# Six leading up-projection units instead of four, earlier squares of the second rows, and GpSimd's two-input sums on VectorE

## The chip, the cores and the metric

One core of one Trainium2 chip runs the whole kernel. The metric is the device time of one execution in microseconds. Before the change it is 2574.07 us (median of three runs, 2573.06 to 2575.15). The engines are named as the profile names them: PE is TensorE (PEld its weight loads), DVE is VectorE, ACT is ScalarE, POOL is GpSimd, and SP is SyncE, which issues DMAs.

## The reference

The input x has 2048 positions of 1024 channels, all in float32. There is one layer:

```python
xn = rmsnorm(x, norm1_g)
z = xn @ w_in                         # 1024 -> 512 pool + 4 x 512 HGRN2 + 2048 gates
u_pool, zq, zf, zi, zo, zg = split(z)
gates = sigmoid(zg + b_gate)          # two gates of 1024 channels
ya = pool_mixer(u_pool) @ w_pa        # window means of 2, 4, 8, 16 positions minus the token
yb = hgrn2_mixer(zq, zf, zi, zo) @ w_pb    # chunkwise gated linear recurrence
x = x + (gates[0] * ya + gates[1] * yb) @ w_o
h = rmsnorm(x, norm2_g) @ w_up        # 1024 -> 2 x 2816
hc = causal depthwise convolution of h over 3 positions, + conv_b
x = x + (silu(gate half of hc) * value half of hc) @ w_down
return rmsnorm(x, final_g)
```

## The kernel before

**Passes and products.** The 2048 positions are done in two passes of 1024. A pass consists of `mixer` (input projection, pooling, recurrence, the two branch projections and the output projection `wo`) and `ffn` (up-projection, convolution, gate, down-projection `dn`). Within a pass the positions stand in two blocks of 512. Each large matrix product is done in a two-by-two scheme with seven products P1 to P7 instead of eight: the operands are sums and differences of quarters of the weights and of the activations, and the results are added and subtracted again. Every float32 operand is split into a high part that the matmul takes exactly (ACT or POOL: a cast, `hi`) and the rest (DVE: `lo` is the value minus `hi`), and each step is three matmuls (hi with hi, hi with lo, lo with hi).

**A unit.** In the up-projection a unit m computes one tile of 128 value channels and the tile of 128 gate channels that belongs to it, for both blocks. There are 22 units of seven products, and each product has twelve matmuls over 512 columns. A unit uses three PSUM banks: X for P1 and P2, Z for P6, P7 and P4, V for P5 and P3. `Unit.after` (line 1028) takes the results out: after P1 ACT copies `e1` from X (L1031), after P6 DVE makes `u2` from Z (L1033), after P7 DVE makes `u3` from Z (L1037), and the four results of a unit come after P2, P7, P4 and P3. P4 goes on adding to bank Z, so it cannot begin before `u3` has read that bank.

**Which products can begin.** P1 and P2 need only forms of the pass's first block (B11, B21). P6, P5, P7, P4 and P3 need forms that mix both blocks (T2, T1, T3, T4, B22). These are made by `forms_b_task` (line 678): PE turns the rows of the second block, DVE makes the differences t1, t2 (L712), POOL some of the others (L729, L746), ACT and DVE split each into `hi` (L606) and `lo` (L607). The task starts with `norm_rows`: for each row tile, two squares on ACT with a running sum (L635), the root on POOL (L636, L628, L629) and the scaling on DVE (L649). After that it waits for `go`. In the up-projection `go` is given before the sixth product (`GO_AT = 5`). `up_order` (line 426) writes out the order of the products: with `N_HEADS = 2`, the units 0 and 1 and then 2 and 3 do P1 and P2 first (eight products), then each pair its other five; the remaining units follow, interleaved one product of one unit with one of the next.

**Weights.** `Stream.convert` takes the next weight operand from its raw buffer (eight of these, filled by SP), lets ACT cast `hi` (L205) and DVE make `lo` (L206), up to four products ahead and into six buffers. It calls `load_ahead`, which issues the next raw loads.

**After a unit.** Results wait in a list `work`; one item is taken after each product (`drain(1)`). Items are `conv` (POOL copies two columns of history, L1402 and L1404; ACT the first tap, L1407; DVE two more, L1409 and L1412) and `glu` (ACT the activation L1416; then a product of gate and value: L1418 on DVE for the second block, L1420 for the first block, there on POOL for units 0 to 3 and on DVE for the rest). When two neighbouring units are through, `add_forms` makes their four sums or differences for the down-projection on POOL (`comb`, L1103, named gf); each is stored by a DMA that POOL issues too (L1432). In the down-projection they are fetched again by POOL's queue (L805). The output projection gets its sums in the same way (yf) while the second branch projection (`pb`) runs, without a store.

**Other POOL sums that the change touches.** `pool_task` makes the window sums by doubling (L778): groups 0 and 2 on POOL, groups 1 and 3 on DVE. The last norm multiplies one half row tile of the first block by the gain on POOL (L1484).

**Order and buffers.** The program is traced in Python; a scheduler then fixes one order for each engine from the order of tracing and its own estimates, and at run time each engine goes through its list. `behind` adds an edge that the scheduler must keep. Tiles of 128 x 512 share 82 slots. In the head of the kernel the first block's `forms_a_task` is traced, then the loads of the second block's rows; the second block's `norm_rows` (names x1_0 to x1_3) is traced at the first tick of the matmul count, so after the first weight conversions.

Of the kernel before, what the change touches and what calls it, by code (L numbers as in the profile page):

```python
# [14 lines left out]
AF = mybir.ActivationFunctionType  # L15
ALU = mybir.AluOpType
# [42 lines left out]

N_SLOTS = 82  # L60
N_RUN = 3
N_HEADS = 2
GO_AT = 5
LEAD = 5
X_AT, X_AT2 = 1, 4
GO_IO = (("P2", 1), ("P2", 0))
G_POOL = 4
O_AT, O_LAG = 3, 1
FIN_WAIT = 4
N_RAW = 8  # L70
# [8 lines left out]
def tile_trunk(  # L79
# [32 lines left out]
    def f32(ap):  # L112
        return ap.bitcast(F32)
# [43 lines left out]
    class Stream:  # L157
# [34 lines left out]
        def convert(self):  # L192
            j = len(self.tiles)
            key, fn, raws = self.ops[j]
            while any(r.tile is None for r in raws):
                self.load()
            store_kept()
            v = fn(f"w{j}")
            t = opsp.tile([P, 2, 512], F32R, tag="ops", name=f"ops{j}")
            n = int(np.prod(v.shape[1:]))  # L200
            hi, lo = t[:, 0, :n], t[:, 1, :n]
            if len(v.shape) == 3:
                hi = hi.rearrange("p (a b) -> p a b", a=v.shape[1])
                lo = lo.rearrange("p (a b) -> p a b", a=v.shape[1])
            self.mark = act.copy(hi, v)  # L205
            dve.tensor_tensor(lo, v, f32(hi), ALU.subtract)  # L206
            self.tiles.append((key, t))
            self.load_ahead()
# [24 lines left out]
            mybir.DependencyClass.NoSync, mybir.DependencyReason.DATA), reason="behind")  # L233

    urgent = [None]

    def first(ins):

# [182 lines left out]
        return {p: (lambda p=p: plan(p)) for p in ORDER}  # L421

    def up_order():
        heads = [(0, 1), (2, 3), (4, 5)][:N_HEADS]
        res = [(m, p) for ms in heads for p in ("P1", "P2") for m in ms]
        res += [(m, p) for ms in heads for p in ("P6", "P5", "P7", "P4", "P3") for m in ms]

        rest = [(7 * m + 2 * i, m, p) for m in range(2 * N_HEADS, MF)
                for i, p in enumerate(ORDER)]
        return res + [(m, p) for _, m, p in sorted(rest)]  # L430
# [201 lines left out]
    def row_rstd(halves, junk, name):  # L632
        ss = small.tile([P, 4], F32, tag="ssq", name=name + "ss")
        for hf in range(2):
            act.activation(junk[hf], halves[hf], AF.Square, accum_out=ss[:, hf : hf + 1])  # L635
        pool.tensor_tensor(ss[:, 2:3], ss[:, 0:1], ss[:, 1:2], ALU.add)  # L636
        return rstd_of(ss[:, 2:3], 1, 1.0 / D, name + "r")

# [125 lines left out]


    def pool_task(b, g, u, w_mix, md):
        add = pool if g % 2 == 0 else dve
        w = WINDOWS[g]
        pool.tensor_copy(u[:, 1:16], uhist[:, g, 1:16])
        pool.tensor_copy(uhist[:, g, 1:16], u[:, 513:528])  # L770
        s = u
        k = 1
        lo = 1
        while k < w:
            t = slot(f"s{b}_{g}_{k}", 528)
            lo += k
            a = 16 if 2 * k == w else lo
            add.tensor_tensor(t[:, a:528], s[:, a:528], s[:, a - k : 528 - k], ALU.add)  # L778
            s = t
            k *= 2  # L780
            yield 6
        p = slot(f"p{b}_{g}")
        dve.scalar_tensor_tensor(p, s[:, 16:528], 1.0 / w, u[:, 16:528], ALU.mult, ALU.subtract)
        if b == 0:
            dve.tensor_tensor(p[:, :16], s[:, 16:32], inv[:, g], ALU.mult)
            dve.tensor_tensor(p[:, :16], p[:, :16], u[:, 16:32], ALU.subtract)
        pl = split(p, f"pl{b}_{g}")
        yield 6
        ps = bank(f"pm{b}_{g}")
        c = g * P  # L790
        pe.matmul(ps, w_mix[:, 0, c : c + P], pl[0], start=True, stop=False)
        pe.matmul(ps, w_mix[:, 0, c : c + P], pl[1], start=False, stop=False)
        pe.matmul(ps, w_mix[:, 1, c : c + P], pl[0], start=False, stop=True)
        t = slot(f"mx{b}_{g}")
        act.activation(t, ps, AF.Copy, scale=col(o_ps + g))
        md[b, g] = spill(t, f"md{b}_{g}")
# [300 lines left out]
    def add_forms(two, forms, k, name, store=lambda p, t: None, sums=True, pin=lambda i: None):  # L1097

        def comb(p, x0, x1, op):
            if (p, k) in forms or x0 is None or x1 is None:  # L1100
                return
            t = slot(f"{name}_{p}_{k}")
            pin(pool.tensor_tensor(t, x0, x1, op))  # L1103
            forms[p, k] = t
            store(p, t)

# [273 lines left out]
    def ffn(b0, forms, late):  # L1380
# [15 lines left out]
        def emit_up(m):  # L1396
# [17 lines left out]
            def glu(hf):  # L1414
                g = ts[1, hf]
                in_turn(act.activation(g, g, AF.Silu))  # L1416
                if hf:
                    dve.scalar_tensor_tensor(g, g, -1.0, ts[0, hf], ALU.mult, ALU.mult)  # L1418
                else:
                    (pool if m < G_POOL else dve).tensor_tensor(g, g, ts[0, hf], ALU.mult)  # L1420
                k = m // 2
                two = gp.setdefault(k, {})
                two[hf, m % 2] = g
# [45 lines left out]
        def final(hf, j):  # L1469
# [11 lines left out]
            for c in (1 - hf, hf):  # L1481
                if (hf, c) == (0, 1):
                    act.activation(res[c], halves[c], AF.Copy, scale=r[:, 0:1])
                    pool.tensor_tensor(res[c], res[c], fg[c], ALU.mult)  # L1484
                else:
                    dve.scalar_tensor_tensor(res[c], halves[c], r[:, 0:1], fg[c],
                                             ALU.mult, ALU.mult)
# [61 lines left out]
        nxt[1].step()  # L1549
    load_rows(1)  # L1550
    join(nxt[1])
    Task(setup_task())
    lg = cols[:, o_lb : o_lb + 4]
    dve.tensor_tensor(lbt[:, 0], lg, lg, ALU.subtract)
# [61 lines left out]
```

## Time and profile before

| what | value |
|---|---|
| median of three runs | 2574.07 us |
| profiled execution | 2575.64 us, of which the span is 2573.9 us |
| mean granted clock of TensorE | 0.993 |
| head: up to the end of the combined projection `io` | about 0 to 122 us |
| first pass: rest of the mixer, `wo`, up, down | up begins at 651 us, down at 1093 us |
| second pass | from 1312 us; up begins at 1913 us, down at 2347 us |

How to read the profile: the page gives busy times of the engines over the span. The timeline lists instructions in order of time: start in us, duration in us, engine, line, operation, output<-inputs, count, and in brackets the idle time of that engine just before, with what ended it. The windows view gives, for each stretch, busy us and number of instructions of each engine, the granted clock of TensorE (1.00 is full speed), the busy share of the DMA engines and GB/s. The groups view gives busy us and mean ns of all instructions of one line.

### The profile page before, as it was taken

The page shows a single profiled execution, that of the slowest core. Times are in us where ns is not written, and L with a number is a line of the kernel's source. Part 1 is how long each engine was busy: PE and PEld are TensorE (multiplying, and loading weights), DVE is VectorE, ACT ScalarE, POOL GpSimd, SP SyncE. Part 2 cuts the span into 40 slices and gives each one's busy share as a digit, 9 for nine tenths or more (in the row PEclk, how much of TensorE's full clock was granted, in tenths as well). Part 3 has the DMA queues.
Part 4 walks back from the last instruction along what each step waited for, and adds up shares of the span by engine and source line. Part 5 has one row for each costly group of instructions (what it writes and reads, how often), then busy time and mean ns, then how long its engine had stood idle before and what let it go on. Part 6 is the DMA issues. An engine that isn't in the chain of part 4 may idle for free.

```text
span 2573.9 us, 35491 instructions
## 1 busy us (share of the span) xinstructions
PE 2519.3 (98%) x11464; PEld 2057.0 (80%) x11464; DVE 1964.0 (76%) x3382; ACT 1191.9 (46%) x2244; POOL 851.5 (33%) x1209
## 2 busy tenths in 40 slices
PE   7899999999999999999999999999999999999998
PEld 6678888788788888878878888888887888888887
DVE  7878788478789777786486776775978987778844
ACT  5335434324555544554364354442355554445533
POOL 6534344031445333462141111200223433334502
PEclk9899999999999999999999999999999999999999
DMA  6787768767788888887364343356442454446942
GB/s 219 254 248 204 210 201 247 215 223 245 179 235 235 235 242 230 252 318 252 107 211 149 99 139 119 120 160 224 143 165 88 151 153 144 144 139 209 366 149 98
DMA packets 254058, 496.88 MB, mean 193 GB/s; under 512 B 26736, under 2 KB 43248, under 8 KB 253552
## 3 DMA queue, kind: packets, MB, share of 16 engines
q1 hardware_dynamic: 187968, 319.89, 38.5%
q0 software_dynamic: 41504, 110.64, 16.8%
q10 hardware_dynamic: 24400, 64.08, 7.3%
q8 instruction: 90, 1.47, 0.2%
q14 instruction: 96, 0.79, 0.1%
HBM read 384.94 MB, written 187.17 MB: 222 GB/s over the span
## 4 chain that ended last, share of the span: by engine, by line
PE 89%; DVE 5%; issue 2%; ACT 2%; DMA 1%; POOL 1%; SPq 0%; DVEq 0%; POOLq 0%; ACTq 0%
PE dn_P L145 16%; PE up_Z L145 14%; PE up_V L145 9%; PE up_X L145 9%; PE wo_P L145 6%; PE gr_Z L145 5%; PE pb L145 3%; PE pa L145 3%; PE gr_X L145 3%; PE gr_V L145 3%; PE fr_Z L145 3%; PE fr_V L145 2%; PE fr_X L145 2%; PE pl L867 1%; PE io_Z L145 1%
## 5 line engine op out<-in xcount | busy, mean ns | idle before, releaser
L205 ACT CAST ops<-raw 128x512 fp32r<-128x512 f32 x732 | 452.7, 620 | 792.9 <-PE dn_P L145 147.6
L206 DVE TENSOR_TENSOR ops<-raw,ops 128x512 fp32r<-128x512 f32 x732 | 555.4, 762 | 207.8 <-ACT ops L205 204.0
L1409 DVE SCALAR_TENSOR_TENSOR e<-h,cols,e 128x512 f32<-128x512 f32 x176 | 142.4, 812 | 30.8 <-ACT e L1407 26.5
L1407 ACT ACTIVATE e<-h,cols 128x512 f32<-128x512 f32 x176 | 142.4, 814 | 29.1 <-DVE h L997 21.0
L1412 DVE SCALAR_TENSOR_TENSOR e<-h,cols,e 128x512 f32<-128x512 f32 x176 | 133.7, 768 | 2.8
L805 POOL DMA_DIRECT2D g_P<-dg_P x154 | 83.3, 543 | 101.3 <-PE dn_P L145 28.5
L1103 POOL TENSOR_TENSOR gf_P<-e,e 128x512 f32<-128x512 f32 x44 | 65.6, 1493 | 153.3 <-DVE e L1418 98.8
L1103 POOL TENSOR_TENSOR gf_P<-gf_P,e 128x512 f32<-128x512 f32 x44 | 59.1, 1344 | 66.6 <-DVE e L1418 66.1
L1402 POOL COPY h<-h 128x2 f32<-128x2 f32 x88 | 39.5, 463 | 121.2 <-DVE h L995 119.2
L1404 POOL COPY hist<-h 128x2 f32<-128x2 f32 x88 | 38.8, 442 | 121.1 <-DVE h L997 119.4
L1416 ACT ACTIVATE e<-e 128x512 f32<-128x512 f32 x88 | 55.6, 632 | 46.2 <-DVE e L1412 46.0
L997 DVE TENSOR_TENSOR h<-up_u,up_V 128x512 f32<-128x512 f32 x88 | 60.0, 682 | 13.3 <-PE up_V L145 12.8
L1212 POOL TENSOR_TENSOR q<-q,qs 128x512 f32<-128x512 f32 x16 | 22.7, 1419 | 139.0 <-ACT qs L1211 127.9
L854 POOL COPY qm<-q 128x64 f32<-128x64 f32 x64 | 24.4, 404 | 117.7 <-DVE q L860 43.9
L1079 DVE TENSOR_TENSOR x<-x,wo_P 128x512 f32<-128x512 f32 x88 | 56.0, 675 | 8.3 <-PE wo_P L145 8.1
L1249 ACT ACTIVATE gt<-gt,cols 128x512 f32<-128x512 f32 x48 | 34.8, 725 | 57.5 <-DVE gt L997 35.1
L1079 DVE TENSOR_TENSOR ac<-ac,dn_P 128x512 f32<-128x512 f32 x72 | 47.3, 682 | 18.4 <-PE dn_P L145 16.5
L1103 POOL TENSOR_TENSOR yf_P<-ya,ya 128x512 f32<-128x512 f32 x16 | 21.1, 1322 | 117.3 <-DVE ya L1326 117.3
L628 POOL TENSOR_SCALAR ro<-so 128x4 f32<-128x4 f32 x16 | 3.2, 199 | 156.8 <-ACT junk L969 156.8
L1477 POOL TENSOR_TENSOR fss<-fss 128x1 f32<-128x1 f32 x16 | 6.6, 415 | 144.2 <-ACT fo L1467 144.2
L1432 POOL DMA_DIRECT2D dg_P<-gf_P x88 | 50.1, 569 | 8.5 <-POOL gf_P L1103 7.7
L1031 ACT COPY up_e<-up_X 128x512 f32<-128x512 f32 x44 | 25.8, 586 | 57.6 <-PE up_X L145 47.5
(1267 smaller groups left out, 8303.4 us busy)
## 6 DMA issues: line engine op xcount, KB each, us to landing
g_P<-dg_P POOLq DMA_DIRECT2D x154, 256.0 KB, 6.4
raw<-in_w_up_t SPq DMA_DIRECT2D x132, 256.0 KB, 3.1
raw<-in_w_in_t SPq DMA_DIRECT2D x98, 256.0 KB, 3.2
dg_P<-gf_P POOLq DMA_DIRECT2D x88, 256.0 KB, 3.8
raw<-in_w_io SPq DMA_DIRECT2D x68, 256.0 KB, 4.8
dg_P<-e SPq DMA_DIRECT2D x66, 256.0 KB, 3.2
raw<-in_w_dn SPq DMA_DIRECT2D x66, 256.0 KB, 4.5
x<-in_x SPq DMA_DIRECT2D x64, 256.0 KB, 5.1
```

Source lines behind the costliest of these rows:

```text
L145: count[1] = pe.matmul(*args, **kw)
L205: self.mark = act.copy(hi, v)
L206: dve.tensor_tensor(lo, v, f32(hi), ALU.subtract)
L805: eng.dma_start(t, d)
L997: dve.tensor_tensor(dst, t, ps, ALU.add if how == "add" else ALU.subtract)
L1079: dve.tensor_tensor(t, t, ps[j], ALU.add if sg > 0 else ALU.subtract)
L1103: pin(pool.tensor_tensor(t, x0, x1, op))
L1407: in_turn(act.activation(t, h[:, 2:], AF.Identity, bias=col(o_cb + mt), scale=col(o_cw + 4 * MF + mt)))
L1409: in_turn(second(dve.scalar_tensor_tensor(t, h[:, 1 : 1 + TB], col(o_cw + 2 * MF + mt), t, ALU.mult, ALU.add)))
L1412: dve.scalar_tensor_tensor(t, h[:, 0:TB], col(o_cw + mt), t, ALU.mult, ALU.add)
L1416: in_turn(act.activation(g, g, AF.Silu))
L1432: pool.dma_start(d, t)
```

## The change

Four things are changed.

1. `N_HEADS` is 3: units 0 to 5 do P1 and P2 first (twelve products), then each pair its other five. `GO_AT` stays 5.
2. In the head, the second block's `norm_rows` is traced directly after the first block's forms. The first weight operand that takes a used buffer (number 6 and later) gets an edge: its cast on ACT stands behind the last square of x1_3.
3. `comb` in `add_forms` (L1103, 120 instructions), the window sums of groups 0 and 2 (L778, 16), `glu` of units 0 to 3 for the first block (L1420, 8) and the last norm's product (L1484, 8) go from POOL to DVE.
4. Nothing else: the sums of weights, t3 and t4 of the forms, the history copies and all DMAs that POOL issues stay where they are.

```diff
-N_HEADS = 2
+N_HEADS = 3
...
-G_POOL = 4
...
             self.mark = act.copy(hi, v)
+            if j >= N_OPS and opening[0] is not None:
+                behind(self.mark, opening[0])
+                opening[0] = None
             dve.tensor_tensor(lo, v, f32(hi), ALU.subtract)
...
+    opening = [None]
...
-        heads = [(0, 1), (2, 3), (4, 5)][:N_HEADS]
+        heads = [(0, 1), (2, 3), (4, 5), (6, 7)][:N_HEADS]
...
         for hf in range(2):
-            act.activation(junk[hf], halves[hf], AF.Square, accum_out=ss[:, hf : hf + 1])
+            ins = act.activation(junk[hf], halves[hf], AF.Square, accum_out=ss[:, hf : hf + 1])
+            if name == "x1_3":
+                opening[0] = ins
...
-        add = pool if g % 2 == 0 else dve
...
-            add.tensor_tensor(t[:, a:528], s[:, a:528], s[:, a - k : 528 - k], ALU.add)
+            dve.tensor_tensor(t[:, a:528], s[:, a:528], s[:, a - k : 528 - k], ALU.add)
...
-            pin(pool.tensor_tensor(t, x0, x1, op))
+            pin(dve.tensor_tensor(t, x0, x1, op))
...
-                    (pool if m < G_POOL else dve).tensor_tensor(g, g, ts[0, hf], ALU.mult)
+                    dve.tensor_tensor(g, g, ts[0, hf], ALU.mult)
...
-                    pool.tensor_tensor(res[c], res[c], fg[c], ALU.mult)
+                    dve.tensor_tensor(res[c], res[c], fg[c], ALU.mult)
...
     join(nxt[1])
+    nxt[2].step()
     Task(setup_task())
```

## The prediction

> **What bounds the kernel now.** I read the page first, for the engine that fills the span.
>
> ```profile
> span 2573.9 us, 35491 instructions
> PE 2519.3 (98%) x11464; PEld 2057.0 (80%) x11464; DVE 1964.0 (76%) x3382; ACT 1191.9 (46%) x2244; POOL 851.5 (33%) x1209
> ```
>
> PE works in 2519.3 of 2573.9 us, and the change takes no matmul away. So the most that can be won is PE's idle time, 54.6 us, and whatever its busy time loses to a slow clock. The next view is PE's timeline, every row with an idle time that the change can reach, and one row of the chain for the price of a product.
>
> ```profile
> 32.74 0.71 PE L145 MATMUL io_X<-ops,x_f4h 128*128 128x512 f32 x2 [3.00 <-ACT io_e L1142]
> 42.96 1.41 PE L655 MATMUL x_t<-ident,x_xs 128*128 128x128 f32 x9 [0.94 <-DVE x_xs L649]
> 52.31 0.72 PE L145 MATMUL io_Z<-ops,x_T20h 128*128 128x512 f32 x2 [1.78 <-DVE x_t L712]
> 90.08 1.19 PE L145 MATMUL io_Z<-ops,x_T40h 128*128 128x512 f32 x2 [4.31 <-DVE io_u L1148]
> ...
> 679.97 0.51 PE L145 MATMUL up_Z<-m_T23h,ops 128*128 128x512 f32 x1 [1.29 <-ACT m_T23h L606]
> 681.61 0.51 PE L145 MATMUL up_Z<-m_T23l,ops 128*128 128x512 f32 x1 [1.14 <-DVE m_T23l L607]
> 688.29 0.50 PE L145 MATMUL up_V<-m_T11l,ops 128*128 128x512 f32 x1 [0.68 <-DVE m_T11l L607]
> 690.09 0.50 PE L145 MATMUL up_V<-m_T12l,ops 128*128 128x512 f32 x1 [0.84 <-DVE m_T12l L607]
> 700.45 0.47 PE L145 MATMUL up_Z<-m_T40h,ops 128*128 128x512 f32 x1 [0.61 <-DVE up_u L1037]
> 704.89 0.50 PE L145 MATMUL up_Z<-m_T40h,ops 128*128 128x512 f32 x1 [0.47 <-DVE up_u L1037]
> 1108.82 2.13 PE L145 MATMUL dn_P<-ops,dn_P_6h 128*128 128x512 f32 x8 [1.27 <-ACT dn_P_6h L606]
> 1111.42 1.19 PE L145 MATMUL dn_P<-ops,dn_P_6l 128*128 128x512 f32 x4 [0.47 <-DVE dn_P_6l L607]
> 1942.47 0.49 PE L145 MATMUL up_Z<-m_T23h,ops 128*128 128x512 f32 x1 [1.32 <-ACT m_T23h L606]
> 1944.11 0.50 PE L145 MATMUL up_Z<-m_T23l,ops 128*128 128x512 f32 x1 [1.15 <-DVE m_T23l L607]
> 1951.26 0.50 PE L145 MATMUL up_V<-m_T12l,ops 128*128 128x512 f32 x1 [0.30 <-DVE m_T12l L607]
> ```
> ```profile
> 752.34 5.55 PE up_X L145 x24
> ```
>
> Three places stand out: the head, and the start of each up-projection, where PE waits for forms T2 and T1 of the second block. A product of twelve matmuls is 5.55 / 2 = 2.78 us. The windows view shows what such a wait costs on top.
>
> ```profile
> 30.00:40.00 10.00, 7.26 (x25) 5.85 (x26) 6.48 (x11) 5.18 (x14) 9.45 (x23) 0.83 0.56 169
> 680.00:690.00 10.00, 7.44 (x22) 5.07 (x22) 9.77 (x9) 5.77 (x11) 7.08 (x7) 0.83 0.94 180
> 1945.00:1950.00 5.00, 5.00 (x17) 3.92 (x16) 3.96 (x5) 1.80 (x4) 4.35 (x3) 0.66 0.18 56
> ```
>
> The granted clock, next to last but two columns, is 0.83 over 10 us, 0.83 over 10 us and 0.66 over 5 us: (1 - 0.83) x 10 = 1.7 us of full-speed work lost after each of the three stalls, in the last (1 - 0.66) x 5 = 1.7 us again.
>
> The Trainium skill ("TensorE: Matmul & The Clock Gate", "HAM oscillation — how this bites in real kernels") puts the danger at idle gaps beyond about 3.4 us, and so would let the gaps of 1.3 us here go unpunished. By that rule the three times 1.7 us would stay, and my sum below would be 5.1 us smaller; the rows above show the slow clock behind these short gaps, so I go by the rows.
>
> **Part 1: six units lead.** P6 of units 0 and 1 now comes after twelve products instead of eight, while `go` still comes before the sixth. The forms get 4 x 2.78 = 11.1 us more before PE needs the first of them. The four waits for T2 and T1 in the first pass add up to 1.29 + 1.14 + 0.68 + 0.84 = 3.95 us, the three in the second to 1.32 + 1.15 + 0.30 = 2.77 us; 11.1 us covers both, and the DVE and ACT work that makes the forms is the same, spread over more matmul time. With them goes one slow-clock stretch of 1.7 us in each pass. What is late next is the pair of waits for `u3` (0.61 and 0.47 us): P7 of a pair's first unit and its P4 are one product apart, so this depends on where L1037 stands in DVE's list. Three pairs instead of two have this place in a pass; I add 0.54 us, the mean of the two waits, for the third. Gains: 3.95 + 1.7 - 0.54 = 5.1 us in the first pass, 2.77 + 1.7 - 0.54 = 3.9 us in the second. Ends: nothing, if the forms are merely made later; 3.95 + 0.61 + 0.47 + 1.7 = 6.7 us and some 5.5 us, if `u3` comes in time too.
>
> **Part 2: the squares of the second rows.**
>
> ```profile
> 10.88 5.08 SPq L504 DMA_DIRECT2D x<-in_x  x8
> 24.93 0.62 ACT L205 CAST ops<-raw 128x512 fp32r<-128x512 f32 x1 [6.69 <-PE io_X L145]
> 27.13 0.63 ACT L635 ACTIVATE x_xs<-x 128x512 f32<-128x512 f32 x1
> 31.42 0.62 ACT L635 ACTIVATE x_xs<-x 128x512 f32<-128x512 f32 x1
> 32.03 1.53 ACT L1142 COPY io_e<-io_X 128x512 f32<-128x512 f32 x3
> ```
> ```profile
> x<-in_x SPq DMA_DIRECT2D x64, 256.0 KB, 5.1
> ```
>
> The eight squares run on ACT from 27.13 to 32.03 us, 4.9 us, and the copies of `e1` stand behind them, so that P2 begins 3.00 us late. ACT was idle for 6.69 us before the cast at 24.93: that is the cast the new edge puts behind the squares. The second rows' loads are issued from 10.88 to 15.96 us and land 5.1 us after issue by the median, so the last is there at about 21 us (an estimate from these two rows), and 4.9 us of squares fit between 18.2 and 24.9 us. Behind the waiting cast on ACT stand two turned tiles, the next cast and then the `e1` copies; the cast loses nothing, as PE released its buffer only at 24.93. POOL's roots and DVE's scaling of these rows come earlier with the squares. The next two waits in the list, 0.94 for scaled rows and 1.78 for the t2 of the forms, hang on the same chain. The wait of 4.31 at 90.08 is for DVE's `u3`, at the end of a stretch in which DVE has no rest; if DVE's chain does not move as far as PE does, this wait takes back what P2 won. I take the wait removed and its slow clock, 3.00 + 1.7 = 4.7 us. Ends: 0 if the wait at 90.08 grows by all of it, and 4.7 + 0.94 + 1.78 = 7.4 us if the chain moves along.
>
> **Part 3: 152 sums from POOL to DVE.** The price on both engines, and how they meet, is in these rows (counts of the groups, min/median/max in ns for the one line).
>
> ```profile
> L1103 POOL TENSOR_TENSOR gf_P<-e,e x44: 1285/1295/3540, 734.3 to 2365.3; 128x512 f32<-128x512 f32 x44
> L1420 DVE TENSOR_TENSOR e<-e,e x36: 678/685/694, 781.5 to 2364.4; 128x512 f32<-128x512 f32 x36
> L206 DVE TENSOR_TENSOR ops<-raw,ops 128x512 fp32r<-128x512 f32 x732 | 555.4, 762 | 207.8 <-ACT ops L205 204.0
> 683.08 4.55 DVE L206 TENSOR_TENSOR ops<-raw,ops 128x512 fp32r<-128x512 f32 x1
> ```
>
> DVE gets 120 + 16 + 8 + 8 = 152 instructions of 0.685 us, 104 us, and would stand at 1964 + 104 = 2068 us, 80% of the span. It gets something back: the same subtraction that normally takes some 0.685 us has a mean of 0.762 and took 4.55 us once, while POOL ran three sums in a row. (0.762 - 0.685) x 732 = 56 us of DVE's time in this one group is such stretching, and about half of POOL's large sums leave. So DVE's net load grows by some 104 - 28 = 76 us or less (an estimate). Whether that reaches PE is read from the tight stretches.
>
> ```profile
> 535.00:555.00 20.00, 20.00 (x88) 16.23 (x87) 19.33 (x23) 3.52 (x6) 11.75 (x8) 1.00 0.68 217
> 555.00:570.00 15.00, 15.00 (x67) 12.19 (x66) 10.28 (x15) 2.04 (x4) 7.99 (x7) 1.00 0.71 254
> 570.00:610.00 40.00, 40.00 (x175) 32.50 (x174) 39.69 (x65) 20.06 (x36) 5.05 (x4) 1.00 0.66 173
> 850.00:900.00 50.00, 50.00 (x218) 40.58 (x217) 39.25 (x57) 25.00 (x40) 17.65 (x27) 1.00 0.82 224
> ```
>
> In the regular up-projection DVE is busy 39.25 of 50 us. Four sums per two units, that is per 14 products or 38.9 us, are 2.74 us, so 3.5 us per 50: 43 of 50, and PE stays ahead. In the `pb` stage and behind it, it is tight: 16 sums are 11.0 us, and DVE's free time between 535 and 570 is 0.67 + 4.72 = 5.4 us, with 570 to 610 full. By mere addition DVE comes 5.6 us late into `wo`. But its 23 instructions between 535 and 555 took 19.33 us, 0.84 each instead of 0.685: 3.6 us of stretching, which leaves with POOL's sums, and as much again can be expected of the rest to 575. I take 0 here; the end on the other side is 5.6 us and a slow clock of 1.7.
>
> The Trainium skill ("SBUF — State Buffer", "Who interferes with whom") says that a DVE instruction with two SBUF inputs and a GpSimd instruction that reads SBUF exclude each other and that the later one blocks fully. By that rule each sum that leaves GpSimd gives DVE back up to its 1.3 us where the two met, and this stage costs nothing, so the total is as below; by addition it would be 7.3 us longer. The 4.55 us of a single subtraction agree with the rule.
>
> POOL's stores (L1432, 88) now wait for a DVE sum instead of POOL's own. Behind them in POOL's list stand history copies (L1402, L1404), and DVE's second and third taps wait for those; in the regular stage DVE has 7 us of rest in 50 to take this up, so I price it at nothing. POOL's fetches for the down-projection (L805) get a freer queue. At the start of the first `dn`, PE waited 1.27 + 0.47 us for splits that came late, with DVE and POOL sums around them: I take 1.0 of the 1.74 us, with 0 and 1.74 as ends. Window sums, the early `glu` and the last norm are 32 instructions under matmuls; 0.
>
> **Sum.** 5.1 + 3.9 + 4.7 + 1.0 = 14.7 us. The profiled execution took 2575.64 us, the span and 1.7 us around it, and would take 2560.9. It lies 1.57 us above the median of the runs shown; from that median, the forecast is 2574.07 - 14.7 = 2559.4 us.
>
> **Rivals.** (a) The head gives nothing: PE arrives at 85.8 us earlier, DVE's list does not, and the wait of 4.31 us grows by 4.7. For it: DVE is full in that stretch. Against it: the work that moves forward is at the front of that very list. Then 2559.4 + 4.7 = 2564.1.
> (b) DVE becomes the bound around `wo` in the first pass, 5.6 + 1.7 us: 2566.7. The second pass has more room there.
> (c) The lead does not help, because the scheduler, knowing that P6 is later, puts the forms later too; the waits keep their size. Only head and `dn` remain: 2574.07 - 5.7 = 2568.4. If the head fails as well, it is 2573, no change that can be told.
> (d) Slower: the slots run out. The forms of a pass are 7 x 4 x 2 = 56 tiles through the whole up-projection, which leaves 26 of 82. Six leading units hold an `e1` and a result each, 12 instead of 8, and a pair in its later products holds some 8 results and 4 to 8 gate tiles and sums until their stores have landed. That is 24 to 28. Past 26, the `e1` copy on ACT waits for a store, and P2 of that unit, one or two products later, waits on bank X. With a landing time of 3.8 us and a slow clock of 1.7 us per wait, and three such waits in each pass, that is 33 us instead of the 9.0 of the lead: 2574.07 - 5.7 + 33 = 2601. For it:
>
> ```profile
>   POOL gf_P L1103: 7.1, 4
> dg_P<-gf_P POOLq DMA_DIRECT2D x88, 256.0 KB, 3.8
> ```
>
> The `e1` copies (L1031) already wait four times for a POOL sum, 7.1 us in all. Against it: PE shows no wait behind these, and sums that take 0.685 us leave their slots sooner. One wait in a pass would leave a gain; it decides from two in each pass on.
>
> **How the numbers follow.** The forecast has a chance of 0.57, (a) 0.14, (b) 0.09, (c) 0.12, half of it with the head failing too, (d) 0.08. About 0.2% (5 us) is what a measurement of this kernel can tell from no change. Faster by more than that: the forecast, (a), (b) and a part of (c), 0.80; the same: the rest of (c) and a mild (d), 0.13; slower: 0.07. The range goes down to 2551 us (the upper ends of the head, 2.7, of both leads, 1.6 + 1.6, and of `dn`, 0.7, and a little of the 4.31) and up to 2570, past (b) and the first half of (c).
>
> **What would show it.** Right: no idle time before P2 of `io` and before T2 and T1 in both up-projections, the granted clock at 1.00 in the first 50 us of each, the squares before 25 us on ACT, DVE's subtractions (L206) under 0.75 us on average, DVE at about 2000 to 2040 us and POOL down by some 200 us. Wrong: a longer wait for `u3` near 85 us, waits of `wo` for DVE around 590 us, ACT's `e1` copies waiting for stores with PE waiting on bank X behind them, or new waits for L1037 of more than a microsecond in the lead.

## The result, and the profile after

The changed kernel takes 2557.51 us (median of four executions, 2556.46 to 2558.77), the kernel before 2574.19 us (four, 2573.06 to 2575.15). The ratio is 0.9936, with a 95% interval of 0.9918 to 0.9953: 16.7 us faster, where 14.7 were forecast (2559.4). The profiled execution of the changed kernel took 2557.09 us, its span 2555.2 us, at a mean granted clock of 0.996. Lines below 200 keep nearly their old numbers, later ones have moved: L1031 is now L1035, L1037 is L1041, L1103 is L1107, L712 is L717, L206 is L208, L1079 is L1083.

The page after, the same two lines as shown of before:

```profile
span 2555.2 us, 35460 instructions
PE 2513.3 (98%) x11464; PEld 2053.7 (80%) x11464; DVE 1972.7 (77%) x3534; ACT 1189.7 (47%) x2244; POOL 642.6 (25%) x1057
```

PE's idle time fell from 54.6 to 41.9 us and its busy time, with the same matmuls, from 2519.3 to 2513.3: less of it ran at the slow clock. DVE has 152 instructions more and is busy only 8.7 us longer, while POOL lost 208.9 us.

PE's timeline after, the rows with an idle time at the places that the prediction listed (start, duration, instruction, in brackets the idle time before it and what ended it):

```profile
39.08 0.76 PE L660 MATMUL x_t<-ident,x_xs 128*128 128x128 f32 x2 [1.72 <-DVE x_xs L654]
46.66 0.66 PE L660 MATMUL x_t<-ident,x_xs 128*128 128x128 f32 x4 [0.70 <-DVE x_t L717]
47.93 0.66 PE L660 MATMUL x_t<-ident,x_xs 128*128 128x128 f32 x4 [0.61 <-DVE x_t L717]
50.04 0.73 PE L144 MATMUL io_Z<-ops,x_T20h 128*128 128x512 f32 x2 [1.46 <-DVE x_t L717]
86.89 1.19 PE L144 MATMUL io_Z<-ops,x_T40h 128*128 128x512 f32 x2 [3.34 <-DVE io_u L1152]
...
676.15 0.50 PE L144 MATMUL up_X<-m_f4h,ops 128*128 128x512 f32 x1 [0.24 <-ACT up_e L1035]
699.22 0.47 PE L144 MATMUL up_Z<-m_T40h,ops 128*128 128x512 f32 x1 [0.54 <-DVE up_u L1041]
703.71 0.51 PE L144 MATMUL up_Z<-m_T40h,ops 128*128 128x512 f32 x1 [0.46 <-DVE up_u L1041]
1096.86 2.10 PE L144 MATMUL dn_P<-ops,dn_P_6h 128*128 128x512 f32 x8 [1.27 <-ACT dn_P_6h L609]
1311.14 0.71 PE L144 MATMUL io_X<-ops,x_f4h 128*128 128x512 f32 x2 [0.34 <-ACT io_e L1146]
```

The wait of 3.00 us before P2 of `io` is gone, and so is every wait for T2 and T1 in the first up-projection; the second has none either (its largest is 0.56 us, for `u3`). At the start of the down-projection 1.27 us is left and the 0.47 behind it is gone. The first product of the second pass, shortly ahead of the last row, no longer waits; before, PE waited there for DVE's `ac` (L1079):

```profile
1312.53 0.70 PE L145 MATMUL io_X<-ops,x_f0h 128*128 128x512 f32 x2 [1.58 <-DVE ac L1079]
```

The prediction did not have that one. In the head, new waits of 1.72, 0.70 and 0.61 us stand where 0.94 stood.

The windows view after, in three stretches where it was shown of before (from:to, length, then busy us and instructions of PE, PEld, DVE, ACT and POOL, the granted clock, the DMA share, GB/s):

```profile
30.00:40.00 10.00, 8.18 (x39) 6.35 (x38) 8.34 (x15) 1.71 (x4) 9.46 (x20) 1.00 0.81 267
680.00:690.00 10.00, 10.00 (x45) 8.05 (x44) 6.65 (x11) 5.03 (x10) 0.00 (x0) 1.00 1.05 284
1945.00:1950.00 5.00, 5.00 (x24) 4.05 (x23) 5.00 (x6) 2.81 (x5) 3.31 (x2) 1.00 0.12 41
```

The clock is 1.00 in all three, where it was 0.83, 0.83 and 0.66. POOL is as full as before between 30 and 40 us. ACT and POOL in the head, from their timelines, show why:

```profile
18.90 0.67 ACT L638 ACTIVATE x_xs<-x 128x512 f32<-128x512 f32 x1
23.20 0.65 ACT L638 ACTIVATE x_xs<-x 128x512 f32<-128x512 f32 x1
25.06 1.32 ACT L204 CAST ops<-raw 128x512 fp32r<-128x512 f32 x2 [1.12 <-PE io_X L144]
27.84 2.66 ACT L1146 COPY io_e<-io_X 128x512 f32<-128x512 f32 x4 [1.46 <-PE io_X L144]
```

```profile
27.49 1.62 POOL L341 TENSOR_TENSOR w8s<-raw,raw 128x512 f32<-128x512 f32 x1
...
30.90 0.56 POOL L632 TENSOR_TENSOR x_0r<-x_0r,neghalf 128x1 f32<-128x1 f32 x1
...
31.51 1.28 POOL L341 TENSOR_TENSOR w9s<-raw,raw 128x512 f32<-128x512 f32 x1
...
36.03 0.59 POOL L632 TENSOR_TENSOR x_3r<-x_3r,neghalf 128x1 f32<-128x1 f32 x1
```

The eight squares run from 18.90 to 23.9 us, and the `e1` copies are no longer behind them. But the last root comes at 36.03 us, twelve after its square: POOL does weight sums (L341) and masks (L578 to L582) in between. Before, it came at 40.20:

```profile
40.20 0.54 POOL L629 TENSOR_TENSOR x_3r<-x_3r,neghalf 128x1 f32<-128x1 f32 x1
```

So the squares end 8.2 us earlier (23.9 against 32.0), the roots come 4.2 us earlier, and the second rows are now late by POOL.

Single profiles differ from one another by chance: a wait for `gr_u` near 460 us is 2.37 us before, 0 after, and between 0 and 3.32 us in the twelve kernels below, whatever they change; the stage around it, from `fr` to `pa`, takes 349.1 to 357.1 us. So I cut all fourteen profiles at the first matmul of each stage and average the kernels that have a part against those that have not. A kernel that changes the stage in another way is left out of its row: the roots ahead of the masks in the head, the later forms and the eight leading units in the up-projection, `comb` or the last norm back on POOL in the down-projection.

| stage | without the part, us (profiles) | with it, us (profiles) | gain | forecast |
|---|---|---|---|---|
| head, start to `fr`: squares | 113.4 (5: 112.1 to 114.6) | 110.9 (8: 110.2 to 111.6) | 2.5 | 4.7 |
| first up-projection: six lead | 434.9 (4: 434.3 to 435.6) | 428.9 (7: 428.3 to 429.7) | 6.0 | 5.1 |
| second up-projection: six lead | 434.0 (4: 432.8 to 435.4) | 428.9 (7: 427.5 to 429.8) | 5.1 | 3.9 |
| first down-projection, to the next pass: sums | 227.5 (4: 227.2 to 228.2) | 224.6 (8: 224.2 to 225.5) | 2.9 | 1.0 |

The four gains add up to 16.5 us, the time fell by 16.7. Of the other stages only `wo` moves clear of its spread, and against the change: 81.4 to 81.7 us in the nine kernels with `comb` on DVE, 81.2 to 81.3 in the five with it on POOL, without a wait of PE in any of them.

For the lead the profiles also say what the gain is made of. Averaged over the same kernels, PE's idle time in the first up-projection falls from 5.8 to 1.8 us and the work lost to the slow clock from 1.7 us to nothing, 5.7 of the 6.0 us; in the second, 4.4 falls to 1.9 and 2.1 to nothing, 4.7 of the 5.1 us. What is left of the stage without waits and slow clock is 425.1 to 428.0 us in all profiles.

### The profile page after: what moved, and what is told of

The parts are those of the page before. It is cut to its first block, busy times and chain, and to the rows that moved or that the text cites. A ratio compares the mean times of both kernels' runs of the same rounds, so it can differ in the third digit from the quotient of the medians.

```text
span 2555.2 us, 35460 instructions
## 1 busy us (share of the span) xinstructions
PE 2513.3 (98%) x11464; PEld 2053.7 (80%) x11464; DVE 1972.7 (77%) x3534; ACT 1189.7 (47%) x2244; POOL 642.6 (25%) x1057
## 4 chain that ended last, share of the span: by engine, by line
PE 55%; DVE 1%; ACT 0%; POOL 0%; issue 0%; DVEq 0%; POOLq 0%; ACTq 0%
PE dn_P L144 16%; PE up_Z L144 7%; PE up_V L144 5%; PE up_X L144 5%; PE wo_P L144 3%; PE gr_Z L144 3%; PE gr_X L144 2%; PE pb L144 2%; PE pa L144 2%; PE gr_V L144 2%; PE fr_Z L144 1%; PE io_Z L144 1%; PE fr_X L144 1%; PE io_V L144 1%; PE fr_V L144 1%; PE pl L871 1%
## 5 line engine op out<-in xcount | busy, mean ns | idle before, releaser
L208 DVE TENSOR_TENSOR ops<-raw,ops 128x512 fp32r<-128x512 f32 x732 | 515.4, 707 | 201.5 <-ACT ops L204 197.1
L1413 DVE SCALAR_TENSOR_TENSOR e<-h,cols,e 128x512 f32<-128x512 f32 x176 | 130.9, 748 | 33.7 <-ACT e L1411 26.1
L1416 DVE SCALAR_TENSOR_TENSOR e<-h,cols,e 128x512 f32<-128x512 f32 x176 | 131.4, 747 | 2.5
L1408 POOL COPY hist<-h 128x2 f32<-128x2 f32 x88 | 45.0, 513 | 161.3 <-DVE h L1001 159.9
L1001 DVE TENSOR_TENSOR h<-up_u,up_V 128x512 f32<-128x512 f32 x88 | 60.0, 682 | 11.2 <-PE up_V L144 11.1
L1083 DVE TENSOR_TENSOR x<-x,wo_P 128x512 f32<-128x512 f32 x88 | 56.2, 680 | 12.3 <-PE wo_P L144 12.0
L1083 DVE TENSOR_TENSOR ac<-ac,dn_P 128x512 f32<-128x512 f32 x72 | 47.3, 681 | 22.0 <-PE dn_P L144 21.7
L1420 ACT ACTIVATE e<-e 128x512 f32<-128x512 f32 x88 | 55.5, 630 | 14.2 <-DVE e L1416 13.5
L1035 ACT COPY up_e<-up_X 128x512 f32<-128x512 f32 x44 | 25.8, 587 | 46.1 <-PE up_X L144 44.6
L871 PE MATMUL pl<-qm,k 128*128 128x192 f32 x256 | 45.4, 326 | 0.3 <-DVE qm L862 0.3
L871 PEld LDWEIGHTS pl<-qm,k 128*128 128x128 f32 x256 | 42.7, 190 | 2.5 <-issue 0.7
```

Source lines behind the costliest of these rows:

```text
L871: pe.matmul(pa_[:, c * 192 : c * 192 + 192], ks[:, (i + c) * P : (i + c + 1) * P], mv[:, c].rearrange("p s x -> p (s x)"), start=True, sto ...
L1001: dve.tensor_tensor(dst, t, ps, ALU.add if how == "add" else ALU.subtract)
L1083: dve.tensor_tensor(t, t, ps[j], ALU.add if sg > 0 else ALU.subtract)
L1413: in_turn(second(dve.scalar_tensor_tensor(t, h[:, 1 : 1 + TB], col(o_cw + 2 * MF + mt), t, ALU.mult, ALU.add)))
L1416: dve.scalar_tensor_tensor(t, h[:, 0:TB], col(o_cw + mt), t, ALU.mult, ALU.add)
```

## The experiments

**Theory A** is the prediction's: each part works by itself, the lead by giving T2 and T1 time, the squares by freeing the `e1` copies, the sums at the start of `dn`. The rivals are named with the runs. The kernels ran in three groups, each beside the kernel before: the lead, the sums, the squares alone and the two pairs (2573.61 us); the later forms, the eight units, the change without its squares and the roots ahead of the masks (2574.14); the quicker pace, the 78 slots, `comb` and the last norm on POOL (2573.27). A ratio compares the means of the executions, so it can differ a little from the medians given.

**Only the lead.**

```diff
-N_HEADS = 2
+N_HEADS = 3
-        heads = [(0, 1), (2, 3), (4, 5)][:N_HEADS]
+        heads = [(0, 1), (2, 3), (4, 5), (6, 7)][:N_HEADS]
```

> The kernel before with N_HEADS = 3 alone. Theory A (each part gains on its own, the lead by giving the T forms 11 us more): no wait for T2 or T1 in either up-projection, each up-projection 4 to 6 us shorter, 2563 to 2566 us in all. Rival B (the starts of the up-projections got faster because the sums on GpSimd no longer block VectorE; the lead adds little): waits for T2 stay, at most 3 us gained, 2571 us or more. Rival C (slots run out while GpSimd still makes the sums slowly): the e1 copies wait for stores, PE waits for bank X, slower than 2574 us.

Measured: 2563.15 us, ratio 0.9963 (0.9951 to 0.9976), 9.5 us less by the ratio and 10.5 by the medians. The up-projections take 428.8 and 429.8 us. The windows of this kernel at the two places of the slow clock:

```profile
680.00:690.00 10.00, 10.00 (x45) 8.11 (x44) 6.67 (x8) 3.65 (x7) 1.94 (x2) 1.00 1.14 267
1945.00:1950.00 5.00, 5.00 (x23) 3.97 (x23) 3.58 (x7) 2.79 (x6) 0.24 (x1) 1.00 0.38 125
```

PE is busy throughout at full clock, with no sum moved. A holds; the lead needs nothing of the other parts.

**Only the sums.**

```diff
-G_POOL = 4
+G_POOL = 0
-        add = pool if g % 2 == 0 else dve
+        add = dve
-            pin(pool.tensor_tensor(t, x0, x1, op))
+            pin(dve.tensor_tensor(t, x0, x1, op))
-                    pool.tensor_tensor(res[c], res[c], fg[c], ALU.mult)
+                    dve.tensor_tensor(res[c], res[c], fg[c], ALU.mult)
```

> The kernel before with the 152 sums moved to VectorE alone. Theory A: the waits for T2 and T1 stay as they are; gains only where VectorE was blocked, that is the wait before gr_Z at 463 us (2.4 us and its slow clock 1.7) and the start of the first down-projection (1.7 to 3 us), about 2567 to 2570 us. Rival B: also the starts of the up-projections, 2562 us or less. Rival D (VectorE becomes the bound around the output projection): 2574 us or more, with waits of wo for VectorE near 590 us.

Measured: 2572.00 us, ratio 0.9994 (0.9985 to 1.0003): not told apart from no change. The first down-projection takes 224.3 us, 3 less, and the waits of 0.47 and 1.58 us are gone; DVE is busy for 1973.9 us. A is missed by 2 us: the wait near 463 us on which it counted stayed, with 2.07 us. The stage table says what is there, this time alone does not.

**Only the squares.**

```diff
             self.mark = act.copy(hi, v)
+            if j >= N_OPS and opening[0] is not None:
+                behind(self.mark, opening[0])
+                opening[0] = None
...
+            ins = act.activation(junk[hf], halves[hf], AF.Square, accum_out=ss[:, hf : hf + 1])
+            if name == "x1_3":
+                opening[0] = ins
...
     join(nxt[1])
+    nxt[2].step()
     Task(setup_task())
```

> The kernel before with the second rows' squares in front alone. Theory A: P2 of io begins without a wait, VectorE's chain moves by less than PE does, and 3 to 4 us remain at the end of the head, 2570 to 2571 us. Rival E (the head is bound by VectorE's chain alone): the wait near 86 us takes everything back, 2574 us. Rival F (the rest of the head follows, with the wait at 463 us too): 2567 us or less.

Measured: 2572.69 us, ratio 0.9996 (0.9988 to 1.0005), less than A said and again within noise, so that the time alone does not exclude rival E. The profile speaks against E: the wait near 86 us is 3.02 us and not longer, and the head takes 110.2 us, where the five kernels without the squares take 112.1 to 114.6. The first Z product of `io` starts at 50.1 instead of 52.3 us.

**The change with two pairs.**

```diff
-N_HEADS = 3
+N_HEADS = 2
```

> The changed kernel with N_HEADS = 2, so everything but the lead. Theory A: the waits for T2 and T1 return, 9 to 10 us above the changed kernel, 2566 to 2568 us. Rival B: within 3 us of the changed kernel, 2557 to 2560 us.

Measured: 2568.88 us, ratio 0.9980 (0.9971 to 0.9989), 0.9 us above A's upper end. The up-projections are back at 434.3 and 434.2 us.

**Six units, the other forms four products later.** This gives the forms no more time than before, though the order of products is the new one.

```diff
-N_HEADS = 2
-GO_AT = 5
+N_HEADS = 3
+GO_AT = 9
```

> The kernel before with six leading units, and the other forms started four products later (GO_AT 9 in place of 5), so that they again have the same number of products ahead of their first reader as in the kernel before. Theory A (the lead works by giving the forms T2 and T1 time: seven products of 2.7 us in place of three): the waits of about 1 us each for T2 and T1 come back in both up-projections, each up-projection is again 433 to 435 us long, and the time is 2571 to 2575 us. Rival B (the lead works by its order of products alone, for instance by the distance between a unit's P1 and the products that read e1, or by weights read ahead): the up-projections stay at 429 to 430 us and the time at 2562 to 2565 us.

Measured: 2568.73 us (its executions range from 2566 to 2575), ratio 0.9987 (0.9978 to 0.9996) where the lead alone had 0.9963. PE's timeline and the windows:

```profile
682.03 0.50 PE L145 MATMUL up_Z<-m_T23h,ops 128*128 128x512 f32 x1 [1.30 <-ACT m_T23h L606]
683.65 0.50 PE L145 MATMUL up_Z<-m_T23l,ops 128*128 128x512 f32 x1 [1.13 <-DVE m_T23l L607]
...
1945.05 0.51 PE L145 MATMUL up_Z<-m_T23h,ops 128*128 128x512 f32 x1 [1.29 <-ACT m_T23h L606]
1946.70 0.50 PE L145 MATMUL up_Z<-m_T23l,ops 128*128 128x512 f32 x1 [1.15 <-DVE m_T23l L607]
```

```profile
680.00:690.00 10.00, 7.57 (x26) 5.25 (x24) 8.53 (x10) 4.44 (x9) 5.71 (x5) 0.83 0.57 187
1945.00:1950.00 5.00, 3.80 (x11) 2.76 (x12) 4.73 (x5) 2.63 (x5) 5.00 (x5) 0.76 0.16 52
```

The waits for T2 are those of before to a few hundredths (1.29, 1.14, 1.32, 1.15), and the slow clock is back with them; the up-projections take 432.9 and 432.2 us, so that of the 11.1 us by the table 7.4 are lost (865.1 us for both, 857.7 with the lead, 868.9 without). The rival, that the order alone does it, falls. A's time of 2571 to 2575 is missed by 2.3 us: of the waits for T1 only 0.30 us came back in the first pass, against 1.52 before. The rest of the difference is the scatter of PE's work between profiles: the waits and the slow clock of both up-projections together are 13.1 us before, 3.6 with the lead alone and 11.9 here.

**The change with eight leading units.**

```diff
-N_HEADS = 3
+N_HEADS = 4
```

> The changed kernel with eight leading units in place of six. Theory A (with six, the waits for T2 and T1 are gone altogether, and a fourth pair has nothing left to take): the up-projections stay at 428 to 430 us, 2556 to 2560 us. Rival C (each leading pair holds more e1 tiles and results, and the 82 slots are nearly used up): waits for slots at e1 copies or forms, up-projections 2 us longer or more, 2562 us or more.

Measured: 2563.97 us, ratio 0.9964 (0.9952 to 0.9977). That is 6 us worse than with six, as the rival on slots said; but look at what PE waits for, and at DVE just before:

```profile
1975.88 0.77 PE L144 MATMUL up_Z<-m_T40h,ops 128*128 128x512 f32 x1 [3.33 <-DVE up_u L1041]
```

```profile
1973.85 0.68 DVE L610 TENSOR_TENSOR m_T43l<-m_t,m_T43h 128x512 fp32r<-128x512 f32 x1
1974.45 0.68 DVE L610 TENSOR_TENSOR m_B223l<-m_b,m_B223h 128x512 fp32r<-128x512 f32 x1
1975.05 0.68 DVE L1041 TENSOR_TENSOR up_u<-up_Z,up_e 128x512 f32<-128x512 f32 x1
```

`u3`, which frees bank Z, is queued behind the last splits of T4 and B22. The same wait of 3.33 us stands at 718.45 in the first pass. The task that makes the forms goes by the count of products: the four splits of T1 are five ticks apart, 20 ticks or ten products, unless a product needs them sooner. With eight units P6 comes so late that nothing hurries the task.

**The same with a quicker pace.**

```diff
             forms["T1"].append(split(t1[k], f"{name}T1{k}"))
-            yield 5
+            yield 2
```

> Eight leading units as in the run before, with the pace of the splits of T1 set to two ticks each in place of five (they take 8 ticks, four products, instead of 20). Theory J (with eight units nothing is short of slots; the other forms are merely made at a pace that puts the splits of T4 and B22 in front of u3 in VectorE's list, and PE's wait of 3.33 us for u3 in each up-projection comes from there): that wait falls under 1 us in both passes, the up-projections are 428 to 430 us, 2556 to 2560 us. Rival C (slots run out with eight leading units): the wait for u3, or one for a slot, stays, 2562 us or more.

Measured: 2557.85 us, ratio 0.9938 (0.9926 to 0.9951). The waits of 3.33 us are gone, the up-projections take 428.8 and 428.0 us. Theory J holds; the lateness was pace, not slots. A fourth pair brings nothing beyond the third.

**The change with 78 slots.**

```diff
-N_SLOTS = 82
+N_SLOTS = 78
```

> The changed kernel with 78 slots in place of 82. Theory A (slots don't bind with six leading units; some are left): the up-projections stay at 428 to 430 us, 2556 to 2560 us. Rival C (the 82 slots are nearly used up by the six units): four slots less bring waits of e1 copies or forms, the up-projections grow by 2 us or more each, 2562 us or more.

Measured: 2558.92 us, ratio 0.9939 (0.9927 to 0.9952), up-projections 429.1 and 427.5 us. Four slots fewer cost nothing that can be told: the prediction's rival (d) is refuted.

**The change without its squares** (the third diff undone).

> The changed kernel with the squares of the second rows back where they were (six leading units and the sums on VectorE stay). Theory A (each part works by itself): the lead's 10.5 us and the sums' 1.6 us, 2560.5 to 2562.5 us. Rival G (the lead and the sums help each other, so that together they give more than the two alone, and the squares give next to nothing): 2556.5 to 2559 us.

Measured: 2562.03 us, ratio 0.9952 (0.9939 to 0.9964), as A said and above the rival's 2559. The squares are then worth about 4 us on top of the other two parts, so G falls. The times of the parts alone add up to 12.0 us by their ratios (9.5, 1.5 and 1.0, each uncertain by 2 to 3) against 16.5 together (uncertain by 4.5); so the times leave room for some help of one part for another. The stages give no sign of it: alone, each part shortens its own stage to what it takes with the others, the head to 110.2 us, the up-projections to 428.8 and 429.8, the first down-projection to 224.3.

**The roots ahead of the masks.**

```diff
         dve.reciprocal(flat_inv, flat_inv)
-        yield 1
+        yield 8
```

> The changed kernel with the masks of the setup made some seven products later, so that GpSimd's roots of the second rows stand ahead of the masks. Theory H (after the squares moved, the roots on GpSimd are what the second rows are late by: x_3r came at 36 us though its squares ended at 24 us): the roots come 3 us earlier or more, PE's wait of 1.72 us at 39 us goes, the stage to the first Z product of io is 1.5 to 3 us shorter, 2554.5 to 2556.5 us. Rival I (the first products of the other forms then wait for the weights' sums or casts in their place): the wait stays or moves, 2557 to 2559 us.

Measured: 2556.66 us, ratio 0.9934 (0.9922 to 0.9947), not told apart from the change's 0.9936. In PE's timeline of this kernel the head does get shorter:

```profile
36.87 0.33 PE L660 MATMUL x_t<-ident,x_xs 128*128 128x128 f32 x1 [0.93 <-DVE x_xs L654]
...
46.79 1.20 PE L144 MATMUL io_Z<-ops,x_T20h 128*128 128x512 f32 x2 [1.46 <-DVE x_t L717]
```

The wait of 1.72 us is 0.93, the first Z product starts 3.25 us earlier, and the head takes 108.3 us, under all eight others with the squares. Of the 3.25 us, 1.25 are there before the roots matter, as the first product of `io` starts at 15.68 instead of 16.93 us. The last root starts at 33.76 us, 2.3 earlier, not 3 as H had it; two weight sums still stand ahead of it. The size of the first wait proves little: it is 0.87 us in the kernel with eight leading units too, whose head is that of the change. That POOL's roots were next late fits this one profile; the times do not show the gain.

**The 120 sums of `comb` back on POOL.**

```diff
-            pin(dve.tensor_tensor(t, x0, x1, op))
+            pin(pool.tensor_tensor(t, x0, x1, op))
```

> The changed kernel with the 120 sums of the down- and the output projection (comb) back on GpSimd; window sums, unit products and last norm stay on VectorE. Theory K (of the sums, those for the down-projection are what paid: the wait of 0.47 us ahead of its first products and the wait of 1.58 us at the boundary of the passes): the first down-projection takes 227 us again in place of 224.5, 2559 to 2562 us. Rival L (the boundary wait is due to the last norm's products, which stay on VectorE here): the first down-projection stays under 225.5 us, 2557 to 2559 us.

Measured: 2560.55 us, ratio 0.9943 (0.9929 to 0.9956); the first down-projection takes 226.2 us, between what K and L said. The page's line of engines, and PE at the start of `dn` and at the pass boundary:

```profile
PE 2512.5 (98%) x11464; PEld 2052.8 (80%) x11464; DVE 1973.4 (77%) x3414; ACT 1189.8 (47%) x2244; POOL 817.8 (32%) x1177
```

```profile
1100.30 1.20 PE L144 MATMUL dn_P<-ops,dn_P_6l 128*128 128x512 f32 x4 [0.98 <-DVE dn_P_6l L610]
...
1299.68 0.70 PE L144 MATMUL io_X<-ops,x_f0h 128*128 128x512 f32 x2 [0.24 <-DVE ac L1083]
```

The wait for the split of `dn_P_6` is back with 0.98 us, as K said; the one at the boundary is not (0.24), as L said. And DVE does 120 sums fewer than in the changed kernel yet is busy 0.7 us longer.

**The eight products of the last norm back on POOL.**

```diff
-                    dve.tensor_tensor(res[c], res[c], fg[c], ALU.mult)
+                    pool.tensor_tensor(res[c], res[c], fg[c], ALU.mult)
```

> The changed kernel with the eight products of the last norm back on GpSimd, all other sums on VectorE. Theory K: the first down-projection stays under 225.5 us and the time at 2556 to 2559 us. Rival L (the last norm on GpSimd runs beside the next pass's first forms and holds VectorE's accumulation there): the wait of 1.6 us for ac at the pass boundary is back, the first down-projection takes 226 us or more, 2558 to 2561 us.

Measured: 2560.79 us, ratio 0.9948 (0.9936 to 0.9961); the first down-projection takes 226.4 us. PE's timeline of this kernel:

```profile
1301.05 0.70 PE L144 MATMUL io_X<-ops,x_f0h 128*128 128x512 f32 x2 [1.62 <-DVE ac L1083]
```

The boundary wait is back, from four products in this pass: rival L holds. The path is not the one that L had in mind. SP's and DVE's timelines of this kernel:

```profile
1273.11 3.24 SPq L507 DMA_DIRECT2D x<-in_x  x5
```

```profile
1297.70 1.60 DVE L654 TENSOR_SCALAR x_xs<-x,x_3r 128x512 f32<-128x512 f32 x2 [0.44 <-POOL x_3r L632]
1299.22 1.09 DVE L610 TENSOR_TENSOR x_f0l<-x_b,x_f0h 128x512 fp32r<-128x512 f32 x1
1300.23 0.67 DVE L1083 TENSOR_TENSOR ac<-ac,dn_P 128x512 f32<-128x512 f32 x1
```

and of the changed kernel:

```profile
1269.92 1.40 SPq L507 DMA_DIRECT2D x<-in_x  x3
```

```profile
1293.60 1.56 DVE L654 TENSOR_SCALAR x_xs<-x,x_3r 128x512 f32<-128x512 f32 x2
1295.08 0.67 DVE L610 TENSOR_TENSOR x_f0l<-x_b,x_f0h 128x512 fp32r<-128x512 f32 x1
1295.68 0.68 DVE L1083 TENSOR_TENSOR ac<-ac,dn_P 128x512 f32<-128x512 f32 x1
```

POOL does roots and products of the last norm in turn, so the products (1.29 us each) delay the next roots; the stores of `fo` wait for both; the next pass's row loads stand behind these stores in SP's queue and are issued 3.2 us later, of which 1.5 us were there when the down-projection began and 1.7 came with the products; so the rows are scaled later, and the `ac` that frees PE's bank stands behind that scaling in DVE's list. That every link is needed was not tried one by one.

## Why the prediction was right, and where it was not

**The forecast and its side.** 16.7 us came where 14.7 were forecast, by the mechanism forecast for the lead and in part for the rest. That the sum came so near is partly luck: by the stage table the lead and the sums gave 2.1 and 1.9 us more than forecast, the squares 2.2 less. Rivals (a) to (d) did not come: the wait of 4.31 us near 90 us became 3.34, no longer one; `pb` and `wo` show no new wait of 1 us; the forms were not put later; the slots were not near their end. Rival (c) is just what the run with the forms four products later does. In the chances, the forecast, (a) and (b) add up to the 0.80 for faster by themselves (0.57 + 0.14 + 0.09), although the prediction names a part of (c) with them.

**The lead: right, a little small.** 9.0 us forecast, 11.1 by the stage table, 9.5 by the time of the lead alone. The waits for T2 and T1 and their slow clock went, as worked out. The term that was wrong is the 0.54 us taken off in each pass for a third `u3` place: after the change there are still only two such waits (0.54 and 0.46 us). With four pairs the same place did cost 3.33 us, for the reason named in that step: where L1041 stands in DVE's list.

**The squares: right in mechanism, mis-sized.** 4.7 us forecast, 2.5 found. The wait of 3.00 us went, but the step that let the rest of the chain follow held only by half: "POOL's roots and DVE's scaling of these rows come earlier with the squares". The squares ended 8.2 us earlier, the last root was taken 4.2 us earlier. POOL's weight sums and masks were queued between them; the prediction counted the queue of ACT and not POOL's. So 1.72 and then 0.70 and 0.61 us came in place of 0.94. Nor did the slow clock go each time with the wait: the head loses 1.7 to 6.8 us to it in the eight profiles with the squares (4.3 on average) and 3.4 to 6.8 in the five without (6.1).

**The sums: right side, small, one place missed.** 1.0 us was taken for the start of `dn`, out of 1.27 + 0.47 us of wait. The 1.27 us stayed in every kernel (1.34 in one); the second wait is 0.47 us before, 0.84, 0.84 and nothing in the three other kernels that keep all sums on POOL, and 0.98 in the run with `comb` on POOL. So the place was right, and the term about twice too large. Most of the rest of the 2.9 us is the boundary of the passes, where the last norm was priced at 0 as "32 instructions under matmuls". The instructions were under matmuls; what stood behind them, stores, then loads in SP's queue, then DVE's `ac`, was not followed.

**DVE's load: mis-sized, without harm.** Forecast: 2000 to 2040 us busy. Measured: 1972.7. 152 sums of 0.685 us are 104 us; DVE got 95 back, not 28, because what it did beside POOL's sums was shorter. The weight subtractions alone (732) went from 555.4 to 515.4 us. The groups views, a row of the kernel before and two of the changed kernel:

```profile
L1409 DVE SCALAR_TENSOR_TENSOR e<-h,cols,e 128x512 f32<-128x512 f32 x176 | 142.4, 812 | 30.8 <-ACT e L1407 26.5 <-POOL hist L1404 2.4 <-POOL h L1402 0.5
...
L208 DVE TENSOR_TENSOR ops<-raw,ops 128x512 fp32r<-128x512 f32 x732 | 515.4, 707 | 201.5 <-ACT ops L204 197.1 <-DMA raw<-su4s 0.8 <-DMA raw<-sd2s 0.7
L1413 DVE SCALAR_TENSOR_TENSOR e<-h,cols,e 128x512 f32<-128x512 f32 x176 | 130.9, 748 | 33.7 <-ACT e L1411 26.1 <-POOL h L1406 4.3 <-issue 0.7
```

The prediction counted only that one group of DVE, and half of its stretching; the second of the three convolution taps (142.4 us before, 130.9 here) gave back 11.5 more, and others smaller amounts. The Trainium skill ("SBUF — State Buffer", "Who interferes with whom"), which has such pairs of instructions exclude each other, agrees: by the run with `comb` on POOL, 120 sums cost DVE as much when POOL does them as when DVE does. DVE's 88 sums of one input in SBUF and one in PSUM (L997, now L1001) took 0.682 us before and after, with no stretching to give back.

**The clock.** In nine of the ten up-projections with the waits for T2 (five kernels, two passes) 1.7 us or more of full-speed work was lost behind them; in none of the fourteen of the seven kernels with six leading units and `GO_AT` 5. The Trainium skill's bound of about 3.4 us for harmful gaps ("TensorE: Matmul & The Clock Gate", "HAM oscillation — how this bites in real kernels") does not hold for these: two gaps of 1.3 and 1.1 us within 3 us were enough, while the single gap of 1.27 us at the start of `dn` was followed by none. The traces show what decides. The slow stretches begin on a fixed grid of 3.41 us and last one or two of its steps, at half the clock. The windows view cut on that grid, first for the kernel before, then for the squares alone, the tenth of the ten:

```profile
679.00:682.41 3.41, 1.30 (x4) 0.86 (x5) 3.10 (x5) 2.11 (x4) 3.00 (x4) 1.00 1.10 257
682.41:685.82 3.41, 3.41 (x9) 2.63 (x8) 3.40 (x2) 1.14 (x2) 3.41 (x4) 0.50 0.64 89
...
1935.01:1938.42 3.41, 2.48 (x11) 1.69 (x9) 3.31 (x4) 1.42 (x3) 1.21 (x2) 1.00 0.25 77
1938.42:1941.84 3.42, 1.97 (x7) 1.42 (x8) 3.09 (x4) 2.40 (x6) 3.42 (x4) 1.00 0.24 81
1941.84:1945.25 3.41, 3.41 (x16) 2.48 (x14) 3.40 (x4) 1.77 (x4) 3.41 (x3) 1.00 0.23 77
```

In the first, both gaps fall into one step, PE is idle for 2.11 of 3.41 us, and the next step runs at 0.50; in the second, gaps of the same length (1.24 and 1.14 us) fall into two steps, with 0.93 and 1.44 us idle, and the clock stays. The fourteen traces have 10272 full-speed steps between 20 and 2540 us: all 44 with 1.82 us or more of PE's idle time are followed by a slow one, none of the 10216 with less than 1.68, and 7 of the 12 in between. So about half a step idle brings the slow clock, and for short gaps it matters where the grid falls, which differs from profile to profile.

## What to carry to other kernels

When a wait for prepared operands stands at the head of a stage, put products that need none of them in front, and give the preparation its start as early as before: the order with a start as many products later gave back two thirds of the gain. An elementwise sum with two SBUF inputs on GpSimd is no relief for VectorE when VectorE is busy beside it; here 120 of them weighed the same on either engine. When an instruction moves to another engine, follow the stores, loads and accumulations queued behind it, and not its own cover alone.

## What the runs showed of the hardware

Two short gaps close together can cost more than their length: 1.30 and 1.13 us were followed by a stretch of 3.41 us at half the clock, 1.7 us more. In these fourteen traces it takes about 1.7 to 1.8 us of idle time in one step of a fixed grid of 3.41 us. And GpSimd's sums take VectorE's time one sum for one: 175 us less of GpSimd (817.8 to 642.6) for 120 more VectorE instructions, some 82 us of work, at no cost to VectorE, whose other instructions became that much shorter.
